# Attention on one Trainium2 core: first row tiles transposed one by one, a later gate for the bulk loads, and V of the second batch loaded over three periods

## Chip, cores and metric

One core of one Trainium2 chip. The metric is the device time in microseconds (us) of one execution. A kernel is judged by the median of several executions, and always beside executions of the kernel before on the same chip.

## The reference

```python
# q, k, v: (8, 2048, 512) float32
scores = np.matmul(q, k.transpose(0, 2, 1)) / np.sqrt(512)
return np.matmul(softmax(scores, axis=-1), v)
```

## The kernel before

Inputs are loaded as float16 in chunks of 512 rows. q and k are transposed, scores are computed with the keys on the partitions, exponentials go to float16 tiles, and a second product with V follows. Both products use a seven-product scheme for 2 x 2 blocks, so DVE must form sums and differences of q, k, V and the exponentials ("background sums"), and each group of scores ends in corrections on DVE. One period is one tile of 512 queries; 32 periods follow each other. The matmul engine (PE) is full nearly throughout. A "bank" below is a part of the memory that PE writes its sums to; dummy matmuls work on zeros and only keep PE busy. The "granted clock" is the share of full speed that the profile records for PE.

The parts that matter here. The start: eight row tiles arrive on the SyncE queue, everything else on the software queue of GpSimd (POOL), behind a "gate", a tiny copy that waits for one of the first rows:

```python
load_first("q", 0, nc.sync, row());   load_first("k", 0, nc.sync, row())
load_first("q", 1, nc.sync, row());   load_first("k", 1, nc.sync, row())
# ... rows 2, 3 of q, then rows 2, 3 of k
nc.gpsimd.tensor_copy(out=gate[:], in_=firsts["k", 0][:, 0:1])
load("k", 0, 1, (2, 2)); load("k", 0, 2)       # chunks 1 and 2 of k
new_v(0); load_v(0, 0)                         # first chunk of V
idle(9)                                        # dummy matmuls
# rows 0, 1 of q and k converted; pairs transposed with idle(1) between,
# then the score halves, with the transposes of rows 2, 3 between
load("k", 0, 3)                                # chunk 3 of k
load("q", 0, 1)
for c in range(1, NCH): load_v(0, c)
```

In each period, 28 slots each hold one score product, and half of them an output product as well. After each slot, one background sum may be taken from a queue, in some slots two ("double pops"):

```python
if background and (g == 0 or slot % len(QORDER) in (0, 2, 3, 6)):
    background.popleft()()
    if background and ((g == 0 and slot in (0, 1, 8, 10, 12, 14, 15, 16, 17, 18))
                       or (0 < g < NQT and slot % 14 == 6)):
        background.popleft()()
```

`Pair.after3` takes a reciprocal on DVE and scales an output half by it on ScalarE (ACT); PE waits for that copy to get its bank back. `Group.after7` and `after3` are corrections on DVE (`cz`), L315 and L318 in this file; products that come later wait for them to free a bank. The changed file is three lines longer there: L315 and L318 of before are L318 and L321 of after, and the score product L292 is L295.

The softmax here doesn't subtract the row's maximum and nothing guards it: scores larger than these inputs give would overflow.

Of the kernel before, what the change touches and what calls it, by code (L numbers as in the profile page):

```python
# [12 lines left out]
def kernel(  # L13
# [21 lines left out]
    nc = tc.nc  # L35
    P = 128
    B, T, D = q.shape
    F16 = mybir.dt.float16
# [6 lines left out]
    ND = D // P  # L45
    QTW = 512
    NQS = QTW // P
    NQT = T // QTW
# [22 lines left out]
    psum = {}  # L71
# [5 lines left out]
    def bank(name):  # L77
        t = psum[name].tile([P, 512], F32, tag=name)
        return t
# [3 lines left out]
    ident = const.tile([P, P], F16)  # L83
# [3 lines left out]
    qT, kT = {}, {}  # L87
    staged = {}
# [9 lines left out]
    def load(what, b, c, pieces=(CH,)):  # L98
        t = staged.get((what, b, c))
        if t is None:  # L100
            t = staged[what, b, c] = stage.tile([P, CH, D], F16, tag="stage", name="stage")
        n = CH - sum(pieces)
        for w in pieces:
            at = c * CH + n
            nc.gpsimd.dma_start(out=t[:, n:n + w, :], in_=srcs[what][b, :, at:at + w, :])
            n += w

    firsts = {}
# [8 lines left out]
    def round_first(what, n):  # L117
        f = nc.vector.tensor_copy if what == "q" else nc.scalar.copy
        f(out=staged[what, 0, 0][:, n, :], in_=firsts[what, n])

    def operands(what):
        pool = kpool if what == "k" else qpool
        raw = pool.tile([P, CH, ND, P], F16, tag=what + "raw")
        sums = [pool.tile([P, 2, 2, P], F16, tag=what + f"s{n}", name=what + f"s{n}") for n in (1, 2, 4)]
        return [raw] + sums

    def dma_transpose(what, b, c):
        src = staged.pop((what, b, c))
        t = operands(what)
        nc.sync.dma_start_transpose(  # L130
            out=t[0][:].rearrange("p n c r -> p (n c) r"),
            in_=src[:].rearrange("p n d -> p (n d)"),
        )
        (kT if what == "k" else qT)[b, c] = t

    def pe_transpose(what, b, c, n0=0, n1=CH):
        src = staged[what, b, c]
        if n0 == 0:
            (kT if what == "k" else qT)[b, c] = operands(what)
        t = (kT if what == "k" else qT)[b, c]  # L140
        for n in range(n0, n1, 2):
            tr = psum["px"].tile([P, 2, ND, P], F16, tag="px", name="tr")
            for m in range(2):
                for dc in range(ND):
                    nc.tensor.transpose(  # L145
                        tr[:, m, dc, :], src[:, n + m, dc * P:(dc + 1) * P], ident[:]
                    )
            if n and c:
                nc.scalar.copy(out=t[0][:, n:n + 2], in_=tr[:])
            else:  # L150
                nc.vector.tensor_copy(out=t[0][:, n:n + 2], in_=tr[:])  # L151
        if n1 == CH:
            staged.pop((what, b, c))

    def k_blocks(t):
        w = t[0][:].rearrange("p (j s) c r -> p j s c r", s=2)
        return w[:, :, 0, 0:2], w[:, :, 0, 2:4], w[:, :, 1, 0:2], w[:, :, 1, 2:4]
# [29 lines left out]
    def new_v(b):  # L187
        vh = vpool.tile([P, NJ, 2, VP], F16, tag="vh")
        t1 = vpool.tile([P, NJ, TP], F16, tag="t1")
        t2 = vpool.tile([P, NJ, H], F16, tag="t2")  # L190
        t4 = vpool.tile([P, NJ, H], F16, tag="t4")
        nc.gpsimd.memset(vh[:, :, 1, D:D + 1], 1.0)
        nc.gpsimd.memset(t1[:, :, H:H + 1], 1.0)
        vs[b] = (vh, t1, t2, t4)

    def load_v(b, c):
        dst = vs[b][0][:].rearrange("p j s d -> p (j s) d")
        ns = slice(c * CH, (c + 1) * CH)
        nc.gpsimd.dma_start(out=dst[:, ns, 0:D], in_=srcs["v"][b, :, ns, :])
# [13 lines left out]
    def new_p(g):  # L213
        left = [ppool.tile([P, NJ, QH], F16, tag=f"left{s}", name=f"left{s}") for s in range(2)]
        right = ppool.tile([P, NJ, 2, QH], F16, tag="right")
        sums = [ppool.tile([P, NJ, QH], F16, tag=f"s{n}", name=f"s{n}") for n in (1, 2, 4)]
        pts[g] = (left, right, sums)

    def exp(out_, in_):
        nc.scalar.activation(out=out_, in_=in_, func=EXP, scale=inv_sqrt_d)  # L220
# [17 lines left out]
    def plain_half(g, j, half):  # L238

        b, qt = divmod(g, NQT)  # L240
        if j == 0 and half == 0:
            new_p(g)
        st = bank("qx")
        kt, qt_ = kT[b, j // G][0], qT[b, qt][0]
        for s in range(2):
            for dc in range(ND):
                nc.tensor.matmul(  # L247
                    st[:, s * QH:(s + 1) * QH], kt[:, 2 * (j % G) + s, dc, :],
                    qt_[:, 2 * half:2 * half + 2, dc, :],
                    start=(s == 0 and dc == 0), stop=(dc == ND - 1), skip_group_check=True,  # L250
                )
        left, right, _ = pts[g]
        if half:
            exp(right[:, j], st[:].rearrange("p (s q) -> p s q", s=2))
        else:
            for s in range(2):
                exp(left[s][:, j, :], st[:, s * QH:(s + 1) * QH])
# [181 lines left out]
    background = deque()  # L439
    PLAN = {}  # L440
# [12 lines left out]
    for qt_ in range(NQT):  # L453
        PLAN.setdefault((qt_, 0), []).append(("load", "q", 3))
        PLAN.setdefault((qt_, 10), []).append(("trans", "q", 3))
        PLAN.setdefault((qt_, 15 if qt_ == 3 else 12), []).append(("sum", "q", 2))
    

    def prefetch(g, slot):
        b, qt = divmod(g, NQT)  # L460
        todo = PLAN.get((qt, slot), [])
        if g == 0:
            todo = [x for x in todo if x[0] != "newv" and x[1] == "q"]
            if slot == 2:
                dma_transpose("q", 0, 2)
            if slot == 9:
                dma_transpose("q", 0, 3)
        elif g == 1:
            todo = [x for x in PLAN.get((0, slot), ()) if x[0] == "newv" or x[1] == "v"] + todo
        for what in todo:  # L470
            bb, c = b + 1, what[-1]
            if what[0] != "newv" and what[1] == "q":
                if not (2 if what[0] == "sum" else NQT) <= g + what[2] < B * NQT:
                    continue
                bb, c = divmod(g + what[2], NQT)
            elif bb >= B:
                continue
            if what[0] == "newv":
                if g == 1:
                    nc.gpsimd.tensor_copy(out=gate[:], in_=pts[g][0][0][:, NJ - 1, 0:1])  # L480
                new_v(bb)
            elif what[0] == "load":
                load_v(bb, c) if what[1] == "v" else load(what[1], bb, c)
            elif what[0] == "trans":
                dma_transpose(what[1], bb, c)
            else:
                background.extend({"k": k_sums, "q": q_sums, "v": v_sums}[what[1]](bb, c))
        if background and (g == 0 or slot % len(QORDER) in (0, 2, 3, 6)):
            background.popleft()()
            if background and ((g == 0 and slot in (0, 1, 8, 10, 12, 14, 15, 16, 17, 18)) or (0 < g < NQT and slot % 14 == 6)):  # L490
                background.popleft()()


# [24 lines left out]
    load_first("k", 3, nc.sync, rest[3])  # L518

    gate = const.tile([P, 1], F32)  # L520
    nc.gpsimd.tensor_copy(out=gate[:], in_=firsts["k", 0][:, 0:1])
    load("k", 0, 1, (2, 2))
    load("k", 0, 2)
    new_v(0)
# [4 lines left out]
    def idle(n):  # L529
        for _ in range(n):  # L530
            nc.tensor.matmul(dummy[:], warm[:, 0:P], warm[:], start=True, stop=True)

    idle(9)
    for n in range(2):
        round_first("q", n)
        round_first("k", n)
    pe_transpose("q", 0, 0, 0, 2)
    idle(1)
    pe_transpose("k", 0, 0, 0, 2)
    idle(1)  # L540
    for n in range(2, 4):
        round_first("q", n)
        round_first("k", n)
    pe_transpose("q", 0, 0, 2, 4)
    plain_half(0, 0, 0)
    pe_transpose("k", 0, 0, 2, 4)
    plain_half(0, 0, 1)
    plain_half(0, 1, 0)
    pe_transpose("k", 0, 1, 0, 2)
    plain_half(0, 1, 1)  # L550
# [38 lines left out]
    def after_slot(g):  # L589
        if g == 0:  # L590
            return {n: [(g, x)] for n, x in zip([9, 11, 13, 16, 17, 18, 19, 21, 23, 25, 26, 27], FIRST)}
        return {2 * n + 1: [(g, x)] for n, x in enumerate(LAST if g == NP - 1 else ORDER)}

    prev = None
    for g in range(NP):
        todo = after_slot(g)
        for slot in range(NS + 4):
            n, at = divmod(slot, len(QORDER))
            old, what = QORDER[at]
# [52 lines left out]
```

## Time and profile before

| | kernel before |
|---|---|
| time, first measurement | 807.62 us (807.18 to 810.37, 3 executions) |
| time, beside the changed kernel | 808.55 us (807.16 to 810.37, 6 executions) |
| span in the profile | 805.3 us, PE busy 796.8 us |
| first load on the software queue issued | 4.48 us |
| chunk 3 of k lands / PE wants it | 20.04 us / 20.50 us |

The prediction shows the lines. Up to 784 us PE loses time in three places: the start, the first period (25 to 49 us), and about 110 us. Another 3.6 of the 8.5 us fall in the last 21.3 us, at the end of the kernel; the change doesn't touch them. A wait of PE elsewhere, or an idle time of another engine, would be no target.

### The profile page before, as it was taken

The page shows a single profiled execution, that of the slowest core. Times are in us where ns is not written, and L with a number is a line of the kernel's source. Part 1 is how long each engine was busy: PE and PEld are TensorE (multiplying, and loading weights), DVE is VectorE, ACT ScalarE, POOL GpSimd, SP SyncE. Part 2 cuts the span into 40 slices and gives each one's busy share as a digit, 9 for nine tenths or more (in the row PEclk, how much of TensorE's full clock was granted, in tenths as well). Part 3 has the DMA queues.
Part 4 walks back from the last instruction along what each step waited for, and adds up shares of the span by engine and source line. Part 5 has one row for each costly group of instructions (what it writes and reads, how often), then busy time and mean ns, then how long its engine had stood idle before and what let it go on. Part 6 is the DMA issues. An engine that isn't in the chain of part 4 may idle for free.

```text
span 805.3 us, 18442 instructions
## 1 busy us (share of the span) xinstructions
PE 796.8 (99%) x7243; PEld 704.8 (88%) x7243; DVE 589.8 (73%) x1473; ACT 570.9 (71%) x1039; POOL 72.2 (9%) x117
## 2 busy tenths in 40 slices
PE   8999999999999999999999999999999999999998
PEld 5788888888888888888888888888888888888887
DVE  4967886787767778677777777777777777766653
ACT  5767767767767777677677677677777776776773
POOL 4030103000030000300003000110002001000000
PEclk9999999999999999999999999999999999999999
DMA  9949986999479892998929997299972998921112
GB/s 225 196 89 186 211 157 114 207 152 182 95 127 216 147 174 72 153 213 150 155 79 159 209 153 155 64 184 184 180 145 64 190 200 156 158 69 46 54 40 79
DMA packets 190246, 116.56 MB, mean 145 GB/s; under 512 B 124496, under 2 KB 172880, under 8 KB 190160
## 3 DMA queue, kind: packets, MB, share of 16 engines
q0 software_dynamic: 49648, 49.29, 40.2%
q1 hardware_dynamic: 140368, 66.08, 39.1%
q8 instruction: 56, 0.92, 0.5%
q14 instruction: 30, 0.25, 0.1%
q10 hardware_dynamic: 144, 0.03, 0.0%
HBM read 100.70 MB, written 33.55 MB: 167 GB/s over the span
## 4 chain that ended last, share of the span: by engine, by line
PE 95%; DVE 2%; DMA 2%; ACT 0%; issue 0%; SPq 0%; DVEq 0%
PE t L375 48%; PE t L292 45%; DMA raw<-stage 1%; PE t L230 1%; PE tr L145 1%; DMA first<-in_k_dram 1%; PE t L247 0%; ACT o L383 0%; DVE t L209 0%; DVE raw L151 0%; DVE t L207 0%; SPq L115 0%; DVE cz L315 0%; DVE cz L318 0%; DVE raw L171 0%
## 5 line engine op out<-in xcount | busy, mean ns | idle before, releaser
L292 PEld LDWEIGHTS <-raw 128*128 128x128 f16 x1984 | 194.1, 98 | 23.2 <-issue 0.4
L383 ACT ACTIVATE o<-t,r 128x256 f32<-128x256 f32 x256 | 122.2, 477 | 128.2 <-DVE r L403 107.5
L292 PE MATMUL t<-raw 128*128 128x256 f16 x1488 | 203.0, 273 | 0.0
L220 ACT ACTIVATE left<-t 128x512 f16<-128x512 f32 (+1 forms) x264 | 156.7, 594 | 22.3 <-PE t L292 19.7
L375 PEld LDWEIGHTS <-s 128*128 128x128 f16 x1536 | 150.3, 98 | 19.3 <-issue 1.0
L292 PEld LDWEIGHTS <-ks 128*128 128x128 f16 x1488 | 145.6, 98 | 17.8 <-issue 0.8
L386 DVE SCALAR_TENSOR_TENSOR o<-t,r,o 128x256 f32<-128x256 f32 x192 | 92.4, 482 | 83.3 <-PE t L375 47.9
L292 PE MATMUL t<-qs,ks 128*128 128x256 f16 x992 | 139.0, 273 | 0.5 <-ACT t L305 0.4
L220 ACT ACTIVATE right<-cz 128x1024 f16<-128x1024 f32 x124 | 132.6, 1069 | 2.1 <-DVE cz L315 2.1
L375 PE MATMUL t<-t,s 128*128 128x257 f16 (+1 forms) x1024 | 133.0, 273 | 0.0
L375 PE MATMUL t<-vh,left 128*128 128x256 f16 x1024 | 132.7, 273 | 0.0
L309 ACT COPY cz<-t 128x512 f32<-128x512 f32 x124 | 72.7, 587 | 67.6 <-PE t L292 67.3
L375 PEld LDWEIGHTS <-right 128*128 128x128 f16 x1024 | 100.2, 98 | 12.2 <-issue 0.6
L375 PEld LDWEIGHTS <-left 128*128 128x128 f16 x1024 | 100.2, 98 | 11.6
L315 DVE TENSOR_TENSOR cz<-t,cz 128x512 f32<-128x512 f32 x124 | 85.2, 687 | 33.9 <-PE t L292 33.9
L318 DVE TENSOR_TENSOR cz<-t,cz 128x512 f32<-128x512 f32 x124 | 84.8, 684 | 2.1 <-PE t L292 1.9
L292 PE MATMUL t<-qs,raw 128*128 128x256 f16 x496 | 74.4, 273 | 0.2 <-DVE cz L315 0.2
L292 PE MATMUL t<-raw,ks 128*128 128x256 f16 x496 | 74.4, 273 | 0.0
L335 DVE TENSOR_TENSOR s<-right 128x512 f16<-128x512 f16 x128 | 54.0, 422 | 26.8 <-ACT right L220 22.6
L312 ACT COPY cz<-t 128x512 f32<-128x512 f32 x124 | 73.1, 589 | 0.2 <-PE t L292 0.2
L305 ACT COPY t<-t 128x512 f32<-128x512 f32 x124 | 70.7, 570 | 3.0
L375 PE MATMUL t<-vh,s 128*128 128x257 f16 x512 | 66.7, 273 | 0.8 <-ACT o L383 0.8
(47 smaller groups left out, 610.5 us busy)
## 6 DMA issues: line engine op xcount, KB each, us to landing
out_dram<-o SPq DMA_DIRECT2D x127, 256.0 KB, 3.0
vh<-in_v_dram POOLq DMA_DIRECT2D x32, 512.0 KB, 13.9
stage<-in_q_dram POOLq DMA_DIRECT2D x31, 512.0 KB, 12.2
stage<-in_k_dram POOLq DMA_DIRECT2D x30, 512.0 KB, 9.8
raw<-stage SPq DMA_TRANSPOSE x58, 6.8
first<-in_q_dram SPq DMA_DIRECT2D x2, 256.0 KB, 3.2
first<-in_k_dram SPq DMA_DIRECT2D x2, 256.0 KB, 3.8
cz<-in_q_dram SPq DMA_DIRECT2D x2, 256.0 KB, 4.7
```

What stands on the lines that cost most here:

```text
L145: nc.tensor.transpose(tr[:, m, dc, :], src[:, n + m, dc * P:(dc + 1) * P], ident[:])
L220: nc.scalar.activation(out=out_, in_=in_, func=EXP, scale=inv_sqrt_d)
L292: nc.tensor.matmul(dst[:, j * QH:(j + 1) * QH], lhs[:, j, c, :], rhs[:, :, c, :], start=(n in (1, 5) and j == 0 and c == 0), stop=(c == 1) ...
L305: nc.scalar.copy(out=self.y[:], in_=self.x[:])
L309: nc.scalar.copy(out=self.cz[:, :, 1, :], in_=self.two(self.z))
L312: nc.scalar.copy(out=self.cz[:, :, 0, :], in_=self.two(self.x))
L315: nc.vector.tensor_add(self.cz[:, :, 1, :], self.two(self.x), self.cz[:, :, 1, :])
L318: nc.vector.tensor_add(self.cz[:, :, 0, :], self.two(self.z), self.cz[:, :, 0, :])
L335: lambda: add(s1[:, js], a21, a22),
L375: nc.tensor.matmul(dst[:, 0:width], lhs(j), rhs(j), start=(first and j == 0), stop=(j == NJ - 1), skip_group_check=True,)
L383: nc.scalar.activation(out=out_, in_=src, func=COPY, scale=r[:])
L386: nc.vector.scalar_tensor_tensor(out=out_, in0=src, scalar=r[:], in1=out_, op0=MULT, op1=ADD)
```

## The change

The intent is to shorten the three places: at the start each row tile is transposed and copied by itself, so that scores start before all rows are there; in the first period, background sums are put off so that a reciprocal does not stand behind them; half of V's loads of the second batch move to periods 2 and 3. The gate now reads row 1 of q in place of row 0 of k. Words in brackets and dots stand for lines left out.

```diff
@@ the start @@
-    nc.gpsimd.tensor_copy(out=gate[:], in_=firsts["k", 0][:, 0:1])
+    nc.gpsimd.tensor_copy(out=gate[:], in_=firsts["q", 1][:, 0:1])
... 
-    pe_transpose("q", 0, 0, 0, 2)
-    idle(1)
-    pe_transpose("k", 0, 0, 0, 2)
-    idle(1)
-    (rows 2 and 3 of q and k converted)
-    pe_transpose("q", 0, 0, 2, 4)
-    plain_half(0, 0, 0)
-    pe_transpose("k", 0, 0, 2, 4)
-    plain_half(0, 0, 1)
+    first_transpose("q", 0)          # one row tile: 4 transposes, one copy of 512
+    (rows 1 of q and k converted)
+    idle(1); first_transpose("k", 0)
+    idle(1); first_transpose("q", 1)
+    idle(1); (rows 2 converted)
+    first_transpose("k", 1)
+    plain_half(0, 0, 0)
+    (rows 3 converted)
+    first_transpose("q", 2); first_transpose("q", 3); first_transpose("k", 2)
+    plain_half(0, 0, 1)
+    first_transpose("k", 3)
     plain_half(0, 1, 0)
@@ V of the second batch, in prefetch @@
         elif g == 1:
-            todo = [... V of (0, slot)] + todo
+            todo = [... V of (0, slot)] + [x for x in todo if x[1] != "v"]
+        elif g in (2, 3):
+            todo = todo + [x for x in PLAN.get((1, slot), ()) if x[1:] == ["v", g]]
@@ pops @@
-   (g == 0 and slot in (0, 1, 8, 10, 12, 14, 15, 16, 17, 18)) or (0 < g < NQT and slot % 14 == 6)
+   (g == 0 and slot in (0, 1, 9, 15, 16, 17, 18, 19, 20))
```

More of the change, by code (lines that the diff above doesn't have):

```diff
@@ L134, in dma_transpose, with transposed, first_transpose @@
         (kT if what == "k" else qT)[b, c] = t
+    def transposed(what, b, c, n, src, w, copy):
+        if n == 0:
+            (kT if what == "k" else qT)[b, c] = operands(what)
+        t = (kT if what == "k" else qT)[b, c]
+        tr = psum["px"].tile([P, 2, ND, P], F16, tag="px", name="tr")
+        for m in range(w):
+            for dc in range(ND):
+                nc.tensor.transpose(
+                    tr[:, m, dc, :], src[:, n + m, dc * P:(dc + 1) * P], ident[:]
+                )
+        copy(out=t[0][:, n:n + w], in_=tr[:, 0:w])
     def pe_transpose(what, b, c, n0=0, n1=CH):
         src = staged[what, b, c]
-        if n0 == 0:
-            (kT if what == "k" else qT)[b, c] = operands(what)
-        t = (kT if what == "k" else qT)[b, c]
         for n in range(n0, n1, 2):
-            tr = psum["px"].tile([P, 2, ND, P], F16, tag="px", name="tr")
-            for m in range(2):
-                for dc in range(ND):
-                    nc.tensor.transpose(
-                        tr[:, m, dc, :], src[:, n + m, dc * P:(dc + 1) * P], ident[:]
-                    )
-            if n and c:
-                nc.scalar.copy(out=t[0][:, n:n + 2], in_=tr[:])
-            else:
-                nc.vector.tensor_copy(out=t[0][:, n:n + 2], in_=tr[:])
+            transposed(what, b, c, n, src, 2, nc.scalar.copy if n else nc.vector.tensor_copy)
         if n1 == CH:
             staged.pop((what, b, c))
+    def first_transpose(what, n):
+        transposed(what, 0, 0, n, staged[what, 0, 0], 1, nc.vector.tensor_copy)
     def k_blocks(t):
@@ L468, in prefetch @@
         elif g == 1:
-            todo = [x for x in PLAN.get((0, slot), ()) if x[0] == "newv" or x[1] == "v"] + todo
+            todo = [x for x in PLAN.get((0, slot), ()) if x[0] == "newv" or x[1] == "v"] + [
+                x for x in todo if x[1] != "v"
+            ]
+        elif g in (2, 3):
+            todo = todo + [x for x in PLAN.get((1, slot), ()) if x[1:] == ["v", g]]
         for what in todo:
@@ L489, in prefetch @@
             background.popleft()()
-            if background and ((g == 0 and slot in (0, 1, 8, 10, 12, 14, 15, 16, 17, 18)) or (0 < g < NQT and slot % 14 == 6)):
+            if background and ((g == 0 and slot in (0, 1, 9, 15, 16, 17, 18, 19, 20))):
                 background.popleft()()
@@ L533 @@
     idle(9)
-    for n in range(2):
-        round_first("q", n)
-        round_first("k", n)
-    pe_transpose("q", 0, 0, 0, 2)
+    round_first("q", 0)
+    round_first("k", 0)
+    first_transpose("q", 0)
+    round_first("q", 1)
+    round_first("k", 1)
     idle(1)
-    pe_transpose("k", 0, 0, 0, 2)
+    first_transpose("k", 0)
     idle(1)
-    for n in range(2, 4):
-        round_first("q", n)
-        round_first("k", n)
-    pe_transpose("q", 0, 0, 2, 4)
-    plain_half(0, 0, 0)
-    pe_transpose("k", 0, 0, 2, 4)
+    first_transpose("q", 1)
+    idle(1)
+    round_first("q", 2)
+    round_first("k", 2)
+    first_transpose("k", 1)
+    plain_half(0, 0, 0)
+    round_first("q", 3)
+    round_first("k", 3)
+    first_transpose("q", 2)
+    first_transpose("q", 3)
+    first_transpose("k", 2)
     plain_half(0, 0, 1)
+    first_transpose("k", 3)
     plain_half(0, 1, 0)
```

## The prediction

> **What bounds the kernel now.** I began with the page's totals and then asked where the matmul engine is not busy, because only there can a change that keeps the number of matmuls gain anything.
>
> ```profile
> span 805.3 us, 18442 instructions
> PE 796.8 (99%) x7243; PEld 704.8 (88%) x7243; DVE 589.8 (73%) x1473; ACT 570.9 (71%) x1039; POOL 72.2 (9%) x117
> ```
>
> Idle PE time is 805.3 - 796.8 = 8.5 us in all. The view by stretches of time (length, PE busy) tells where:
>
> ```profile
> 0.00:24.50 24.50, 21.16 (x169) 1.00 1.08 222
> 24.50:49.00 24.50, 23.14 (x200) 1.00 0.79 136
> 49.00:98.00 49.00, 49.00 (x451) 1.00 1.12 181
> 98.00:122.50 24.50, 24.32 (x223) 1.00 0.80 156
> 122.50:784.00 661.50, 661.50 (x6055) 1.00 0.78 141
> ```
>
> From 122.5 to 784 us PE has no idle time at all, and the clock granted is 1.00. One query tile (a "period": 28 score products of 4 matmuls and 14 output products of 8, 224 x 0.109 = 24.5 us) follows another at that pace. What is left is 3.3 us at the start, 1.4 us around 25 to 49 us (period 0, the first with output products), and 0.2 us at about 110 us. The change touches exactly these three places. The waits of PE, longest first in total:
>
> ```profile
> PE tr L145 <- DVE stage L119: 1.3, 2, 0.9
> PE t L531 <- DVE warm L504: 1.2, 1, 1.2
> PE tr L145 <- ACT stage L119: 0.8, 1, 0.8
> PE t L375 <- ACT o L383: 0.8, 1, 0.8
> PE t L292 <- ACT t L305: 0.4, 1, 0.4
> PE t L292 <- DVE cz L315: 0.2, 1, 0.2
> ```
>
> The second line is the wait for the first instruction of the program; the change doesn't touch it. The others sum to 3.5 us, which is the ceiling of any gain but for some 0.2 us that each modelled matmul end hides.
>
> **What the Trainium skill says.** "Perfetto Trace Analysis", Optimizing Scalar/DVE Operations, says that where those engines are not saturated but cause bubbles on others, breaking up instructions may let work complete sooner, and that every such instruction has a fixed access overhead. That is the first half of this change; DVE at 73% fits. "VectorE: DVE Perf Modes", Why PSUM operands drop a tier, caps a PSUM copy at two elements per cycle: at 0.96 GHz 0.52 ns each. The copy of 1024 took 0.69 us in the trace, so it agrees (one per cycle would be 1.07), and I estimate the new copy of 512 at 0.69 - 512 x 0.52 ns = 0.42 us. "TensorE: Matmul & The Clock Gate", What's actually happening, says PE runs at half rate until busy for about 3.4 us. The trace agrees: dummy matmuls of 512 columns start every 0.427 us up to 4.6 us and take 0.213 us afterwards; waits of 1 us at 5 to 9 us cost no clock. I expect none with the third dummy.
>
> **Part 1, the start.** Before, two rows at a time are transposed, copied by DVE in one piece, and the first scores follow four rows of q and two of k:
>
> ```profile
> 7.28 0.40 PE L145 MATMUL tr<-ident,stage 128*128 128x128 f16 x4 [0.81 <-ACT stage L119]
> 7.72 0.69 DVE L151 COPY raw<-tr 128x1024 f16<-128x1024 f16 x1 [0.96 <-PE tr L145]
> 8.33 0.75 DVE L119 CAST stage<-cz 128x512 f16<-128x512 f32 x2
> 8.80 0.73 PE L145 MATMUL tr<-ident,stage 128*128 128x128 f16 x8 [0.91 <-DVE stage L119]
> 9.37 1.04 PE L247 MATMUL t<-raw 128*128 128x256 f16 x8
> ```
>
> Row 2 of q, landed at 7.2 us (issue 2.60 plus 4.6), is cast only after DVE has copied k's pair at 8.33; its transpose, in front of the scores on PE, holds them until about 9.4. Three score halves then run without a break and end at 12.52 (16 matmuls at 0.109 from 10.69, with 0.08 between).
>
> After, by the new order, with the landings of the trace (row 1 of k 6.6, row 2 of q 7.2, row 3 of q 7.85, row 2 of k 8.5, row 3 of k 9.2): row 1 of k cast 6.61 to 7.23, transposed 7.28, copied 7.71 to 8.13; the first half's first four matmuls run from 7.5, the other four from 8.17 to 8.61. So the first scores end 1.6 us earlier. But then PE meets new short waits. Rows 2 and 3 of q are transposed by 9.05, copied 9.04 to 9.80; row 2 of k needs the transpose buffer that the first of these copies frees (9.50); the second half waits for the copy of row 3 of q: 9.85 to 10.72. Row 3 of k is transposed 10.72 to 10.94 and copied 11.17 to 11.59; the third half starts on row 2 at once and does its other four matmuls 11.63 to 12.07. Against 12.52 that is 0.45 us, and most of the 1.6 us is given back. If the later gate of the POOL loads (now behind q's row 1, 0.8 us later) lets k's row 1 land sooner than 1.5 us after its neighbour, some 0.15 us more.
>
> A landing caps this. Chunk 3 of k is issued at 9.83 and lands 10.2 later, at 20.03; PE transposes it at 20.50 without waiting. So at most 0.45 us can pass that point, just what I have. The later gate should not move that landing: between 5.95 and 7.9 us the view of the DMA queues shows the hardware queue alone,
>
> ```profile
> q1 hardware_dynamic: 365, 0.67, 103.0%
> ```
>
> so the software loads, issued from 4.48 on, stood behind the rows anyway ("DMA: Bandwidth & Descriptors", Queues, rings and completion order, speaks of round-robin between queues; here the software queue moved nothing while the rows did). **0.45 us.**
>
> **Part 2, period 0.** DVE runs background sums back to back from 24.6, and the reciprocal of the first pair stands in that queue behind two k sums:
>
> ```profile
> 36.92 0.42 DVE L170 TENSOR_TENSOR ks<-raw 128x512 f16<-128x512 f16 x1
> 37.38 0.42 DVE L171 TENSOR_TENSOR raw<-raw 128x512 f16<-128x512 f16 x1
> 37.72 0.16 DVE L403 RECIPROCAL r<-t 128x1 f32<-128x1 f32 x1
> 38.44 1.04 PE L375 MATMUL t<-vh,s 128*128 128x257 f16 x8 [0.78 <-ACT o L383]
> ```
>
> ACT's scaled copy waits for it and PE for that copy. The new double-pop slots (9, 15 to 20 in place of 8, 10, 12, 14 to 18) put both k sums behind the reciprocal: 37.72 - 36.92 = 0.80 us earlier, so PE starts at 37.64; it would be free at about 37.5, so the stall nearly goes. What was put off comes later: the last V difference (L208) is done about 41.65, where its product starts at 41.9; the last L210 about 45.8, where it is wanted at 46.05; the second pair's reciprocal about 46.5, so that its scaled copy ends 47.2, just when PE asks for the bank. I take 0.05 us off. **0.75 us.** The wait on L305 stays: ACT comes to it behind the last exponentials, in the same order as before.
>
> **Part 3, V over three periods.** Two of four V loads move behind the k loads, and their sums to periods 2 and 3; the double pops of periods 1 to 3 go. PE has no idle time in 49 to 98 us, so nothing is to be had there. At 110 us:
>
> ```profile
> 108.42 0.42 DVE L170 TENSOR_TENSOR ks<-raw 128x512 f16<-128x512 f16 x1 [1.01 <-DMA raw<-stage]
> 108.88 0.42 DVE L171 TENSOR_TENSOR raw<-raw 128x512 f16<-128x512 f16 x1
> 109.22 0.68 DVE L315 TENSOR_TENSOR cz<-t,cz 128x512 f32<-128x512 f32 x1
> 109.95 0.60 PE L292 MATMUL t<-qs,raw 128*128 128x256 f16 x4 [0.18 <-DVE cz L315]
> ```
>
> The k sum waits for the chunk's DMA transpose, with the correction PE needs behind it. In the new order that sum is popped at slot 9 rather than 6, some 2.6 us later, by when the transpose has landed. Consecutive PE starts here are 0.34 us beyond the usual pitch (109.18 plus 4 x 0.109 against 109.95). **0.34 us.** The new sums fit: 16 single pops per period for 16 sums, the last V sums in period 4's first slots, before the product that needs them.
>
> **Sum:** 0.45 + 0.75 + 0.34 = 1.5 us. Start and period 0 are in series on PE, and PE runs solid afterwards, so they add. 807.62 - 1.54 = 806.1 us.
>
> **Rivals.** (a) The start gives all back, or more: the small copies and shared transpose buffers take the wait, or chunk 3 of k comes later because the loads are issued 0.8 us later. For it: three new waits above; against: the idle software queue. It makes 806.5, at worst 807.3. (b) Put-off V differences stall PE in period 0 or a late V sum does in period 4: margins there are only 0.2 us; it would return 0.3 to 0.7 us, 806.4 to 806.8. (c) The rows land sooner behind the later gate and PE keeps 1 us of the start if the chunk's landing moves too: 805.5. (d) The traffic was what mattered, and fewer V loads in period 1 speed the kernel: PE's 49.00 of 49.00 us there speaks against it; worth nothing.
>
> **Range and chances.** The three runs before spread from 807.18 to 810.37, so a median may be off by some tenths. Rivals (a) to (c) span 805.2 to 807.3; with the noise I take 804.9 to 807.6. 2% is 16 us; PE's total idle time is 8.5, so faster by that much is out of reach. Slower needs a stall in every period, and the instruction orders are unchanged from period 5 on.
>
> **What would show it.** Right: the first score matmul at about 7.5 us and the third half's end at about 12.1; PE's wait on the scaled copy gone; no wait at 110 us; PE solid after 50 us. Wrong: a wait of PE for a k chunk at 20 us, waits on L208 or L210 at 40 to 46 us, a wait in periods 2 to 4, or a first row of k landing over 0.3 us away from 6.6.

## The result and the profile after

The changed kernel took **809.0 us** (median of 6, 806.96 to 809.27); the kernel before, in the same rounds, 808.55 (807.16 to 810.37). The ratio is 0.9998, 95% interval 0.9977 to 1.0018: the same. Ratios here are the mean time of one kernel's fast runs over that of the other's of the same rounds, so not quite the ratio of the medians quoted. The predicted 1.5 us did not come, and the median lies above the range.

The profiled execution (809.27 us) shows where it went. The waits of PE (engine, tile and line, what was waited for: us in total, times, longest):

```profile
PE tr L143 <- DMA stage<-in_k_dram: 1.4, 1, 1.4
...
PE t L295 <- DVE cz L318: 0.5, 1, 0.5
```

The wait on the scaled copy (0.8 us before) is gone but for some 0.14 us, as foretold. But a wait for a load of k, 1.4 us, has come on top, and one for the correction L318, 0.5 us. By stretches (length, PE busy, clock, DMA share, GB/s):

```profile
0.00:24.50 24.50, 19.98 (x155) 1.00 1.03 206
24.50:49.00 24.50, 23.54 (x199) 1.00 0.86 151
98.00:122.50 24.50, 24.50 (x226) 1.00 0.87 158
```

The start lost 1.2 us of busy time against 21.16 before; the first period won 0.4; the place at 110 us is full. Not foretold are two gaps between PE's starts of 0.22 and 0.21 us at 159 us. There ACT's scaled copy waits until an earlier store of its output buffer has landed (158.50 us). Such gaps, 0.2 to 0.6 us in all, stand in four of the ten profiles with the new plan for V (the changed kernel, E3, E6, E9) and in none of the ten with the old one; no experiment looked into them. The timelines of PE and POOL (start, length, engine, line, what; in brackets the idle time before and its releaser) name the wait and its origin:

```profile
22.29 1.07 PE L143 MATMUL tr<-ident,stage 128*128 128x128 f16 x16 [1.35 <-DMA stage<-in_k_dram]
```

```profile
6.22 0.44 POOL L527 COPY gate<-first 128x1 f32<-128x1 f32 x1 [5.78 <-DMA first<-in_q_dram]
6.60 2.29 POOL L105 DMA_DIRECT2D stage<-in_k_dram  x3
```

Row 1 of q landed at 6.17 us in this execution (5.12 in the kernel before), so the software loads were issued from 6.60 on, 2.1 us later than before, and chunk 3 of k landed at 22.24 in place of 20.04. Yet the first packet of the software queue came only 0.3 us later, at 8.20 in place of 7.91. What fell is the pace after it. GB/s of all queues in 40 slices of 0.65 us from 0 to 26 us, the kernel before, then the changed one; the last row lands at 9.2 and 9.9 us, in slices 15 and 16, and from there on it is the software queue alone but for one packet:

```profile
GB/s 0 0 48 199 398 366 325 296 372 388 331 318 246 208 191 199 202 199 208 211 200 206 206 210 205 206 228 195 197 210 206 205 202 206 211 206 202 208 206 211
```

```profile
GB/s 0 0 50 210 366 337 299 284 280 340 381 413 224 148 189 191 186 154 104 120 139 162 191 184 197 208 206 216 199 206 206 205 205 206 208 205 208 206 203 205
```

Of the prediction's other signs, the first score matmul stood at 8.19 us (about 7.5 foretold) and the third half ended at 12.77 (12.1), with row 1 of k landing at 7.26 instead of 6.6, which the prediction had named as a sign of being wrong.

The theory that I took to the chip: the late gate costs about 1.2 us at chunk 3 of k; the put-off sums give most of Part 2 back at L318; the rest of the change is worth something. Rivals: the rows one by one are themselves no gain; the wait for k comes from the first chunk of V standing ahead in the queue; or the difference is only the spread of executions.

### The profile page after: what moved, and what is told of

Same layout as the page of the kernel before. It is cut to its first block, busy times and chain, and to the rows that moved or that the text cites. A ratio compares the mean times of both kernels' runs of the same rounds, so it can differ in the third digit from the quotient of the medians.

```text
span 807.0 us, 18446 instructions
## 1 busy us (share of the span) xinstructions
PE 797.8 (99%) x7244; PEld 704.6 (87%) x7244; DVE 591.0 (73%) x1477; ACT 570.2 (71%) x1039; POOL 72.5 (9%) x117
## 4 chain that ended last, share of the span: by engine, by line
PE 93%; DMA 4%; DVE 2%; ACT 0%; issue 0%; SPq 0%; DVEq 0%; ACTq 0%
PE t L378 47%; PE t L295 45%; DMA out_dram<-o 2%; DMA stage<-in_k_dram 1%; DMA cz<-in_q_dram 1%; PE t L233 0%; DVE cz L321 0%; PE tr L143 0%; DVE o L389 0%; SPq L115 0%; DVE raw L146 0%; DVE s L338 0%; DVE t L213 0%; DVE right L340 0%; DVE vh L211 0%
## 5 line engine op out<-in xcount | busy, mean ns | idle before, releaser
L318 DVE TENSOR_TENSOR cz<-t,cz 128x512 f32<-128x512 f32 x124 | 85.1, 686 | 34.6 <-PE t L295 34.6
```

The source lines that it names most:

```text
L318: nc.vector.tensor_add(self.cz[:, :, 1, :], self.two(self.x), self.cz[:, :, 1, :])
```

## The experiments

Eighteen runs were made. Medians are given as this / before in the same rounds. "E1" and so on are the numbers in the labels.

### E1: the kernel before, unchanged, as a control

> The kernel before, unchanged, as a null and to see its own spread. Theory A (the pace of the first 15 us of transfers varies from execution to execution, in both kernels): its times fall into two groups some 2 us apart, 807 and 809 to 810, and where the profiled execution is of the upper group, PE waits 1 us or more for chunk 3 of k at about 20 us. Theory B (the later gate of the POOL loads in the changed kernel makes that landing late): the kernel before shows no such wait, and its upper group has another cause. Ratio to the kernel before 1.000 in either case, within 0.15%.

807.9 (806.97 to 815.6) / 807.43 (806.75 to 811.72); ratio 1.0007 [0.9971, 1.0042]. The same kernel spreads over 5 us and more. Its profile shows no wait at 110 us, but PE waits once for chunk 3 of k, which landed at 21.11 us:

```profile
21.16 1.01 PE L145 MATMUL tr<-ident,stage 128*128 128x128 f16 x15 [0.99 <-DMA stage<-in_k_dram]
```

So the landing varies by a microsecond with the early gate too, and the kernel before pays for it in some executions. One profile of before was too little to call 20.04 us a fixed landing: over the twelve profiles with the early gate and the first chunk of V in its old place it lies between 19.30 and 21.11, 20.27 in the mean.

### E2: the changed kernel with the early gate

```diff
-    nc.gpsimd.tensor_copy(out=gate[:], in_=firsts["q", 1][:, 0:1])
+    nc.gpsimd.tensor_copy(out=gate[:], in_=firsts["k", 0][:, 0:1])
```

> The changed kernel with the gate of the POOL loads put back on the first row of k. Theory B: chunk 3 of k lands some 1 us or more earlier than in the changed kernel (22.1 us there), the upper group near 809 goes, and the median falls to about 806. Theory A: the landing still varies by about 2 us with the execution; the two groups stay (about 806.5 and 809), and the median is within 0.1% of the changed kernel's.

806.96 (806.75 to 808.15); 0.998 [0.9956, 1.0003]. One line is worth 1.3 us against the median of the changed kernel's repeat in E5 (808.23), 2.0 against its first one; by the ratios (0.9980 against 0.9995 and 0.9998) it is 1.2 to 1.5. These ran in different rounds, and the intervals overlap; E6 and the landings below make the case. Chunk 3 landed at 20.29 us, and of the wait for k 0.26 us are left (PE's start at 20.33), too little for the view of waits. What is left of PE's waits in period 0 (timeline of PE, then of DVE):

```profile
46.08 0.60 PE L295 MATMUL t<-qs,ks 128*128 128x256 f16 x4
47.14 0.60 PE L295 MATMUL t<-qs,raw 128*128 128x256 f16 x4 [0.46 <-DVE cz L318]
```

```profile
46.08 0.40 DVE L186 TENSOR_TENSOR qs<-raw,qs 128x512 f16<-128x512 f16 x1
46.40 0.68 DVE L318 TENSOR_TENSOR cz<-t,cz 128x512 f32<-128x512 f32 x1
```

DVE works through q sums that the new pops put off and reaches the correction at 46.40; four matmuls that started at 46.08 would have let PE go on at 46.52, and it goes on at 47.14, 0.63 us later than at its usual pitch.

### E3: the late gate kept, the first chunk of V loaded last

```diff
-    load_v(0, 0)                    # after new_v(0)
...
-    for c in range(1, NCH):
+    for c in range(NCH):
```

> The changed kernel with the first V chunk loaded behind chunk 3 of k and the second q tile instead of before them (512 KB, some 2.5 us at the 206 KB/us of the software queue). If the wait for chunk 3 of k is what the upper group is made of (theories A and B alike), that wait is gone in every execution, the groups collapse to a spread under 0.7 us, and the median is about 805.5 to 806. If the upper group remains 2 us above the lower, its cause lies elsewhere. Rival: the V sums at 31 us now wait for their load and give it back: DVE then waits for vh.

807.58 (806.76 to 808.84); 0.9987 [0.9963, 1.0011]. With 512 KB less ahead of it, chunk 3 landed at 19.39 us and its wait is gone. But the median is far from the 805.5 to 806 expected: PE now waits for chunk 2.

```profile
16.80 1.07 PE L143 MATMUL tr<-ident,stage 128*128 128x128 f16 x16 [0.96 <-DMA stage<-in_k_dram]
```

The whole row of loads is late behind the late gate; moving V only decides which chunk shows it.

### E4: the kernel before with the V plan and the pops alone

The `elif g == 1`, `elif g in (2, 3)` and pop lines of the change, nothing else.

> The kernel before with the second half of the change alone: V over three periods and the new double-pop slots, the start untouched. My prediction's parts 2 and 3: the PE wait on the scaled copy at 38 us falls from 0.8 to under 0.1, that at 110 us goes, so the fast executions are 1.1 us below those of the kernel before (806.1 against 807.2) whatever the first loads do. Rival: the put-off sums return it at other places (the changed kernel's trace shows waits of 0.6 us at 48.4 and 0.2 us at 159), and the gain is 0.3 us or less.

807.17 (807.04 to 809.15); 0.9988 [0.9961, 1.0014]. Against 0.94 us before, PE starts 0.15 us late at the scaled copy. But the wait of E2 is here too, 0.63 us at 46.6 us:

```profile
47.32 0.38 PE L292 MATMUL t<-qs,raw 128*128 128x256 f16 x2 [0.47 <-DVE cz L315]
```

So it belongs to the pops, not to the start: of 0.79 us saved, 0.63 is given back, 0.16 us stays. There is no wait at 110 us.

### E5: the changed kernel, unchanged, as a control

> The changed kernel, unchanged, for more executions beside the next ones. If the later gate costs (theory B, which the four profiles so far favour: by 14 us the software queue had moved 1.07 to 1.10 MB with the early gate and 0.77 and 0.85 MB with the late one), at least half of its times lie at 808.5 or above, and the profile shows PE waiting 0.7 us or more on a k load. If it was chance (theory A), most lie at 806.7 to 807.4.

808.23 (807.36 to 808.55) / 808.65 (806.88 to 811.2); 0.9995 [0.9978, 1.0011]: the result repeats. I had expected at least half of the times at 808.5 or above; one of six is. Here row 1 of q landed earlier, the gate let go at 5.42 us, and PE waits for k twice:

```profile
PE tr L143 <- DMA stage<-in_k_dram: 0.9, 2, 0.5
```

### E6: the gate on the last row (k row 3)

```diff
-    nc.gpsimd.tensor_copy(out=gate[:], in_=firsts["q", 1][:, 0:1])
+    nc.gpsimd.tensor_copy(out=gate[:], in_=firsts["k", 3][:, 0:1])
```

> The changed kernel with the gate on the last row of k (lands at 9.2 to 9.9 us), a larger dose of the same thing. Theory B: first software packet at 10.5 or later, chunk 3 of k lands near 23 us in every execution, PE waits some 2.5 us in all for k loads, median 809 to 810, no time under 808.5. Theory A (only the pace of the memory matters, the queue stands behind the rows anyway): median within 0.7 us of the changed kernel's.

810.84 (810.69 to 811.57); 1.0029 [1.0012, 1.0045]. A larger dose of the suspected cause:

```profile
PE tr L143 <- DMA stage<-in_k_dram: 3.9, 3, 2.1
```

Put side by side, first software issue and landing of chunk 3 of k: 4.48 and 20.04 us (before), 5.54 and 20.89 (E5), 6.12 and 21.61 (E8, below), 6.60 and 22.24 (after), 9.86 and 24.87 (E6). A later gate is a later chunk 3, all along this range; only E1's 21.11 with the early gate, 4.43, reaches into it. In E6 all rows had landed (9.69 us) before the first software packet (11.39), and from 14 to 17 us that queue still moved only 93 to 134 KB in each us, so the rows are not what slows it.

### E7: early gate, first chunk of V last, two double pops less

```diff
+    in_=firsts["k", 0]              # the gate, as in E2; V chunk 0 as in E3
-    slot in (0, 1, 9, 15, 16, 17, 18, 19, 20)
+    slot in (0, 1, 9, 15, 16, 17, 18)
```

> The changed kernel with the gate back on k's first row, the first V chunk loaded last of the first loads' k and q, and no double pop at slots 19 and 20. Expected if the three causes are right: no PE wait on any k load (0.26 us with the early gate alone), the 0.6 us wait on the correction at 46.5 us down to under 0.1, the 0.15 at 37 as it was; median 806.2 to 806.5 against 807.2 of the kernel before's fast executions, and few times above 807.5. Rivals: the put-off L213 differences make PE wait for the product at slot 23 (a new wait of 0.3 us or more at 45 us), or the V sums at 31 us wait for their loads.

**805.92** (805.67 to 806.54) / 808.65; 0.9967 [0.9951, 0.9984]. It beats both kernels, by 2.7 us or 0.33% against before. Chunk 3 of k landed at 16.60 us. The stretches (columns as above):

```profile
0.00:24.50 24.50, 21.96 (x178) 1.00 1.08 223
24.50:49.00 24.50, 23.92 (x203) 1.00 0.80 145
```

PE is busy 0.80 us longer in the start and 0.78 us longer in period 0 than in the one profile of the kernel before that the prediction used. Neither L318 nor a load of k is among PE's waits any more.

### E8: the kernel before with the late gate alone

```diff
-    in_=firsts["k", 0][:, 0:1]
+    in_=firsts["q", 1][:, 0:1]
```

> The kernel before with the later gate alone. Theory B: the software queue has moved under 0.95 MB by 14 us, chunk 3 of k lands at 21 us or later, PE waits 1 to 2 us for it, and the median is 1 us or more above the kernel before's of the same rounds. Theory A: same as the kernel before within 0.3 us, the same two groups.

809.99 (808.79 to 812.03); 1.0016 [0.9998, 1.0034]. The interval just includes 1, so the times alone don't prove it. The profile shows the same wait in the old kernel (1.02 us idle at 21.66, chunk 3 landed at 21.61), so it is not a matter of the new row order. Of its 2.5 us over before's first profile (spans 807.8 and 805.3), 1.4 us come from another place, the one at 110 us, here 1.74 us against 0.34:

```profile
112.52 0.60 PE L292 MATMUL t<-qs,raw 128*128 128x256 f16 x4 [1.57 <-DVE cz L315]
```

```profile
110.98 0.42 DVE L170 TENSOR_TENSOR ks<-raw 128x512 f16<-128x512 f16 x1 [2.40 <-DMA raw<-stage]
...
111.78 0.68 DVE L315 TENSOR_TENSOR cz<-t,cz 128x512 f32<-128x512 f32 x1
```

The DMA transpose lands when it lands; the correction behind it makes PE wait anything from nothing (E1) to 1.74 us.

### E9: early gate and two double pops less, V's first chunk in its old place

> The changed kernel with the early gate and without the double pops at slots 19 and 20, the first V chunk where it was: what the pops are worth without the V order. The correction's wait at 46.5 us (0.63 us between PE starts) should be under 0.1; a wait of 0 to 1 us for chunk 3 of k stays and varies. Median 806.2 to 806.8, so 0.4 to 0.6 us under the early gate alone (806.96) and up to 0.8 us over the combined version (805.92). If it equals the combined version, the V order is worth nothing; if it equals the early gate alone, the pops are.

806.49 (806.38 to 806.94) / 808.38; 0.9973 [0.9958, 0.9989]. Against E2 it is 0.47 us less, though in other rounds on another chip and with overlapping intervals. The trace is clearer: the wait at 46 us is gone, as the same place shows:

```profile
46.32 0.60 PE L295 MATMUL t<-qs,ks 128*128 128x256 f16 x4
46.75 0.60 PE L295 MATMUL t<-qs,raw 128*128 128x256 f16 x4
```

The put-off sums were the cause: take the two double pops away and PE goes on at once. What the place of V's first chunk is worth beside it stays unclear: 0.9973 here, 0.9967 in E7.

### E10: the rows one by one alone

The kernel before with the new start, early gate, old V plan and old pops.

> The kernel before with the first rows transposed and copied one by one alone (early gate, V and pops as before). My part 1 without the gate: it reaches chunk 3 of k 0.4 us sooner and then waits for it; against the kernel before's fast executions 0 to 0.4 us. The wait on the scaled copy (0.94 us between PE starts) stays. The V order of the kernel before should bring back the varying wait near 110 us (0, 0.34 and 1.74 us in its three profiles so far, none in the six with the new one), so an upper group at 808.5 to 811 remains in its times. If no time is above 808, the upper group was of the rows' old order and not of that wait.

807.32 (806.84 to 808.0) / 808.38; 0.9983 [0.9967, 0.9999]. The scaled copy's wait is as in before, none at 110 us. The time between PE's starts beyond its pitch of 0.213 us per 512 columns, up to 24.5 us, is 4.62 us against 5.14 before: 0.5 us, near my 0.45. One pair of profiles is little, but the groups stay apart: 4.35 to 5.01 in the five with the rows one by one and the early gate (E2, E7, E9, E10, E12), 5.14 to 5.78 in the kernel before without half clock (before, E1, E14, E16). More striking is that all six executions are at or under 808.0, where before has many over 809. The next experiments turn to that.

### E11: E7 without any gate

> The combined version with no gate at all: the POOL loads are issued from 0.5 us on. If the gate is there to keep them from the first rows, the rows now land later (row 1 of k beyond 7 us), the first scores start 1 us or more later, and the median is 0.5 to 2 us above the combined version. If the loads only queue behind the rows (what my prediction took from the share of the queues), nothing changes, or the k loads land sooner and it is as fast as the combined version.

812.65 (810.95 to 813.77); 1.0047 [1.003, 1.0064], 6.7 us above E7 where 0.5 to 2 was expected. With the software loads free to start at once, row 1 of k landed at 9.92 us where it had been 6.0 to 7.3, and the last row at 15.62:

```profile
PE tr L143 <- DVE stage L119: 2.5, 1, 2.5
```

After it PE ran at half clock for nearly all of 9 to 19 us (granted clock 0.53). So the gate is needed; it must only not be late.

### E12: E7 with the double pops of periods 1 to 3 put back

```diff
-    slot in (0, 1, 9, 15, 16, 17, 18)
+    slot in (0, 1, 9, 15, 16, 17, 18)) or (0 < g < NQT and slot % 14 == 6)
```

> The combined version with the double pops of periods 1 to 3 back (slots 6 and 20), which puts the sums of k's chunk 2 ahead of the correction at slot 8 again, as in the kernel before; loads as in the combined version. The traces say that the chunk's transpose lands no sooner with the new V order (107.4 against 108.4 us, PE itself being 1 us earlier), so it is the place of the sum that took the wait away: a wait of 0.1 to 1.7 us near 108 us comes back, the median rises by 0.2 to 1 us, and the times spread more. If no wait comes back, the V loads' move was what took it away.

806.08 (805.83 to 806.55); 0.9968 [0.9951, 0.9985]. No wait of PE came back near 110 us. But the k sum stands ahead of the correction again, and DVE again idles before it for the DMA transpose (timeline of DVE):

```profile
106.65 0.43 DVE L173 TENSOR_TENSOR ks<-raw 128x512 f16<-128x512 f16 x1 [0.38 <-DMA raw<-stage]
...
107.45 0.68 DVE L318 TENSOR_TENSOR cz<-t,cz 128x512 f32<-128x512 f32 x1
```

With the sum in this old place, PE's wait is this idle time less some 0.66 us: 1.74 us for 2.40 (E8), 0.75 for 1.42 (E16) and 1.41 (E18), 0.63 for 1.29 (E17), 0.34 for 1.01 (before), and none for 0.76 or less (E1, E10, E12 to E15). In the nine profiles with the new pops of periods 1 to 3 (after, E2 to E7, E9, E11), DVE doesn't idle before the sum: in E2 the correction comes first (107.66 us), and the sum at 109.13 finds its transpose landed (107.39). So the place of the sum does make the wait; E12's 0.38 us was too short to reach PE.

### E13 to E16: four more looks at the kernel before

> The kernel before, for its trace. If the upper group is made of the wait near 110 us, an execution above 808.5 us shows 1 us or more there between PE starts, and one below 807.5 under 0.4; if of chunk 3 of k at 20 us, the wait is there instead (1.15 us in the one such trace, of an execution in between).

> As the look before: extra time near 110 us or at 20 us or, if neither, elsewhere in the trace, and then a third cause is needed.

> As the looks before. Of five or more traces of this kernel I expect about half in the upper group and each of these to have 1 us or more near 110 us.

> As the looks before: about an even chance of an execution above 808.5 us, with its extra time near 110 us or at 20 us.

809.27, 807.54, 809.51 and 808.33 us. The two slow ones have no wait at 20 us and none at 110 us. What they have is half rate (stretch, length, PE busy with the number of matmuls, granted clock, DMA share, GB/s; E13, then E14):

```profile
10.00:13.00 3.00, 3.00 (x21) 0.50 1.22 193
```

```profile
10.00:13.00 3.00, 3.00 (x36) 1.00 1.21 199
```

Twenty-one matmuls in 3 us in place of 36. In E13 matmuls ran at full rate by 6.4 us, and at half rate again from 9.35, after waits of 0.80, 0.56 and 0.91 us with short work between:

```profile
6.43 0.40 PE L145 MATMUL tr<-ident,stage 128*128 128x128 f16 x4 [0.80 <-DVE stage L119]
...
10.08 1.92 PE L247 MATMUL t<-raw 128*128 128x256 f16 x8
```

In E15 the matmuls between 5 and 13 us all started at half rate, with a first wait of 1.0 us at 5.4 us, while the record of the clock says 1.00. E16 had the wait at 110 us (0.75 us) instead.

The mean granted clock, recorded for every execution, counts E13's kind without a profile (not E15's, whose record reads 1.00): of 56 executions of the kernel before, 14 have 0.998 or less, and all of these took 808.8 us or longer; 11 others over 809.5 have 1.000. Of 24 executions with the old start otherwise changed (E4, E8, E17, E18), 7 have it. Of 52 executions with the rows one by one and a gate (the changed kernel and E2, E3, E5, E6, E7, E9, E10, E12), none has.

### E17: the kernel before with more dummies after the pairs

```diff
-    idle(1)        # at both places
+    idle(3)
```

> The kernel before with three dummy matmuls in place of one at each of its two places in the start. Theory: the upper group of the times before (809 to 811 us) is largely half clock at 10 to 13 us, granted after three waits of about 1 us at 5 to 9 us; with the waits filled, no execution has half clock there, the times lose that group, and the median is about 807.2, all between 806.7 and 808.5 unless a wait at 20 or 110 us joins. Rival: the half clock has nothing to do with those waits; then one or more of five runs is again over 809, and the median stays within 0.5 us of the kernel before in the same rounds. The dummies may delay a transpose by at most 0.4 us each where a row lands early.

809.29 (807.17 to 813.36) / 808.8; 1.0013 [0.9988, 1.0037]. My theory failed here: two of six executions have a clock of 0.997 and 0.998, and four are over 809. The profile shows a wait of 1.55 us at 5 us, between rows 0 and 1 of q, that these dummies don't fill.

### E18: dummies between rows 0 and 1 of q

```diff
+                if (what, b, c, n, m) == ("q", 0, 0, 0, 0):
+                    idle(3)        # after the four transposes of row 0
```

> The kernel before with three dummy matmuls between the transposes of rows 0 and 1 of q, where the 17th run left an unfilled wait (1.5 us) and where the half clock of two looks began (waits of 1.0 us from 5.4 us on). Theory: the half clock comes from the wait for row 1 of q, which falls on the matmul engine before or just after its clock was raised; filled, no execution has a mean granted clock of 0.998 or less, none has half rate at 10 to 13 us in its profile, and the times keep only what the waits at 20 and 110 us make: median about 807.3, at most one of six over 809. Rival: the waits at 7 to 9 us do it, or another cause; then again about a quarter to a half of the executions have 0.998 or less and times of 809 and more.

807.92 (806.87 to 813.49) / 808.96; 1.0001 [0.9973, 1.0028]. Five of six are at 808.23 or less, one took 813.49 with a clock of 0.998; before, in the same rounds, had 5 of 12 at 0.998 or less. That points towards the first wait, but one remained where I had said none, and six are too few. Which wait lowers the clock is **not settled**.

## Why the prediction was wrong, step by step

**"The later gate should not move that landing" failed.** This is the step of Part 1 that cost most. I had seen that the software queue moved nothing from 5.95 to 7.9 us and took it that a later issue cost nothing as long as it came before 7.9. The reading was right and the inference wrong. With a late gate the queue's first packet came at 7.47 us (E5), 7.62 (E3), 7.65 (E8) and 8.20 (after), against 7.61 to 8.11 with the early one, so the start hardly moved. The pace did: by 14 us the software queue had moved 0.80 MB in the changed kernel, 1.13 in before. E2 takes the delay away and 1.2 to 2.0 us with it, E6 enlarges it, E8 brings the wait into the old kernel (its profile shows it; its time leaves it just unproved), and E3 shows that the whole row of loads is late, not one chunk. In each of the five profiles with a late gate, one of the second to sixth us of the queue moved only 92 to 133 KB; in the fourteen with the early gate none moved less than 153. I had named this as rival (a) and as a sign of being wrong, but gave it "at worst 807.3". Why a later issue slows the queue stays open.

**Part 1's own sum held.** The rows one by one are worth about 0.5 us by E10's profile, for 0.45 predicted; in E2 the third half ends at 12.09 us, and the copies of 512 take 0.42 to 0.43 us in E10, both as worked out. With them the half clock at 10 to 13 us does not appear, in none of 52 executions. I had not seen it, as the one profile I had did not contain it.

**Part 2 was right in its saving and blind to its return.** 0.79 us came off at the scaled copy, as worked out (0.80 predicted, 0.75 taken). But I followed the put-off V differences and the second reciprocal to their uses, and not the correction L318, which stands behind the put-off q sums on DVE. It gave 0.63 us back at 46.5 us. Net 0.16 us in E4 in place of 0.75. E9's trace shows this wait gone with two double pops fewer. This is rival (b) in its mechanism, at an instruction that I had not checked.

**Part 3 was right in its mechanism and mis-sized as a fixed term.** The wait at 110 us is no constant 0.34 us: with the old plan for V it is 0.34, 1.74, 0.75, 0.63 and 0.75 us in five profiles (before, E8, E16, E17, E18) and absent in five (E1, E10, E13, E14, E15), some 0.4 us in the mean; that the single 0.34 came near it was luck. In the ten profiles with the new plan (after, E2 to E7, E9, E11, E12) there is none. That it goes because the sum is popped later is what the traces show (figures at E12): DVE idled before the sum in nine of the ten old profiles and, with the pops put back, in E12, and in none of the nine with the new pops. The sum was popped 2.3 us later by PE's progress (E2 against E1), for 2.6 predicted. PE was not solid afterwards, as the prediction had it: the gaps at 159 us return 0.43 us in the changed kernel.

**The noise was mis-sized.** "Some tenths" was read off three executions. In 56 the kernel before ranged from 806.75 to 815.6 us, with a median of 808.45; the base of 807.62 was on the lucky side by 0.8 us. Its upper part has several causes: the half clock (E13, E15), the wait at 110 us (E16) and the one for chunk 3 of k (E1). The two large errors, about 1.2 us at the gate and 0.6 at L318, are the size of the predicted gain, and the net is the nothing that was measured.

The chances (same within 2%) were right, since 2% is more than all of PE's idle time.

## What to carry to other kernels

Here the gate that holds back bulk loads had to be neither absent nor late: each microsecond later came out as 0.6 to 0.9 us (against the mean landing of 20.27 us) at the chunk that was wanted with least slack, some 15 us afterwards, although the queue's first packet hardly moved. Look at when the last byte lands, not only at when the queue starts. When work is put off on an engine that takes its instructions in order, as DVE does in these timelines, follow every instruction that now stands behind it to its consumer, corrections and bank releases included, not only the put-off work itself. And take more than one profile of the base before calling a wait or a landing fixed.

## What the Trainium skill lacked or had wrong

- "TensorE: Matmul & The Clock Gate", What's actually happening: it lets the clock fall after an idle window of about 3.4 us. Here it fell without a single gap of that length: after waits of 0.80, 0.56 and 0.91 us with transposes and dummies between (E13), and after one of 2.5 us (E11). Further on the page does tell of frequent short idle times that throttle the clock; what it lacks is how little work within a window keeps it, and no run here settles that.
- "DMA: Bandwidth & Descriptors", Queues, rings and completion order: round-robin between queue rows is what E11 looks like (row 1 of k at 9.92 us without a gate, 6.0 to 7.3 with one), but with the gate the software queue moved nothing at 5.95 to 7.9 us while the rows moved, though its loads had been issued from 4.48 on. No page says that loads issued 2 us later also move slower at first (112 to 145 KB per us from 11 to 14 us in the changed kernel, against 200 to 210 in the kernel before).
